# Weight tiles of a two-layer diffusion step: one pump for loads and low parts, and projections' first units loaded inside attention and convolution

## The chip, the core and the metric

One core of one Trainium2 chip runs the whole program. Its engines run in parallel, each through its own stream of instructions in order: TensorE (PE; its weight loads are PEld in the profile), VectorE (DVE), ScalarE (ACT), GpSimd (POOL) and SyncE (SP). POOL and SP also issue DMAs: a DMA that adds to what lies in its destination is issued from POOL. The metric is the device time of one execution in microseconds; lower is better.

## What is computed

Two groups of tokens, 128 of context and 512 of latents, go through two layers; the kernel lays them side by side as 640 columns, features on partitions. A layer is a half-step SwiGLU, a token mixer and a second half-step SwiGLU, each modulated before and normalised after. The mixer of layer 0 is attention (16 query heads, 4 key heads, rotary positions, a window for the latents and a sink), that of layer 1 a Hyena long convolution of order 2.

```python
for i in range(DEPTH):                       # 2 layers
    x = layer_norm(ALPHA*x + 0.5*gate2*swiglu(modulate(x, ...), w1, w2))
    out = attention(modulate(x, ...)) if i % 2 == 0 else hyena(modulate(x, ...))
    x = layer_norm(ALPHA*x + gate5*out)      # out ends in a projection, w_o or w_out
    x = layer_norm(ALPHA*x + 0.5*gate8*swiglu(modulate(x, ...), w1, w2))
# swiglu: (silu(g) * u) @ w2 with g, u = split(h @ w1), inner width 2816
# hyena: h @ w_in (3 parts), short convolution, two long convolutions by FFT, z @ w_out
```

## The kernel before

**Products.** float32 accuracy is had from three products of a faster format (fp32r): a matrix is split into a high part (its rounding) and a low part (the rest), and W x becomes Wh xh + Wh xl + Wl xh. Lines 513 to 524 (`mm_cols`) and 550 to 576 (`ffn1`) issue them in that order, so that the third matmul of every unit is the first that reads the unit's low part. The columns go in two halves of 320.

**Units.** The weights stream through 170 units of 128 partitions and 1 MB (some 768 KB), numbered in the order of use: first feed-forward stage 0 to 35, wqkv 36 to 41 (three for queries, 39 the keys, 40 queries again, 41 the values), wo 42 to 45, feed-forward 46 to 81 and 82 to 117, Hyena input 118 to 129, Hyena output 130 to 133, feed-forward 134 to 169. A feed-forward stage opens with a group of three units (w1) in the order U, U+1, U+2 on half 0 and the same on half 1, and closes with a group of three (one of w1, two of w2b). Between them a w1 unit takes two steps, a w2a unit one. The qkv stage and the Hyena input open with a group of three as well; the two output projections run their first unit alone and the other three as a group.

**Tiles.** The pool `wp` has 8 slots of 1 MB. A unit takes one as it is loaded (`w_dma`, line 108, a DMA from POOL's queue) and a second when its low part is made (`w_split`, line 117): ACT writes minus the high part into the new tile, and a DMA from POOL adds the weights to it from HBM. Both slots come free after the unit's last matmul (`w_done`). Attention puts its key tiles `kh` (two slots) and probabilities `p` (three at a time) into the same pool, the convolution its three tables, its spectra, `ew` and some `yh`, `yl`.

**When.** `run_steps` (line 526) calls `w_get(u)` ahead of every step. Before the change `w_get` issues one more low part whenever fewer than `wmax` units (3) are live and the next one lies at most two ahead, and every low part is followed by loads up to two units further. `wmax` is lowered by hand in attention and convolution, and `wlim` bounds which units may be loaded. The kernel keeps a clock of its own, `now`, which only matmuls of steps advance (0.136 us each); it also places the steps of the layer norms (`at`, `run_due`). In attention both wo units 42 and 43 are loaded before the scores, and 42's low part comes in the group of scores N-3 of N = 20. In the convolution (`hyena`, 8 items of some 8 slots, then a last round with the parts of the projection) unit 130 is loaded at item 7 and its low part made after the fifth slot, followed by the loads of 131 and 132. A program of instructions is written by hand in order, so each engine executes its own in the order of the text.

**Around it.** A residual (`resid`) is a VectorE operation that reads the matmul's result, and from the second column tile on a sum on POOL for the layer norm; the rotary step (`rope`) is ACT, VectorE and POOL work on every q and k tile. `w_first` and `w_split_first` (lines 132 and 140) load a unit on SP's queue as float32 and split it with an ACT copy and a VectorE subtraction; before the change only the first units of all use them.

Of the kernel before, what the change touches and what calls it, by code (L numbers as in the profile page):

```python
# [42 lines left out]
class Kernel:  # L43
# [53 lines left out]
    def w_init(self, units):  # L97
        self.units = units
        self.wd = 0
        self.ws = 0  # L100
        self.wlive = set()
        self.wmax = 3
        self.wlim = len(units)
        self.raw = {}
        self.wt = {}

    def w_dma(self, upto):
        nc = self.nc
        while self.wd < min(upto, self.wlim):
            i = self.wd  # L110
            src, shape = self.units[i]
            r = self.wp.tile(shape, F32R, tag="w", name="wh")
            nc.gpsimd.dma_start(out=r, in_=src)  # L113
            self.raw[i] = r
            self.wd += 1

    def w_split(self):
        i = self.ws
        if i >= self.wlim:
            return  # L120
        self.w_dma(i + 1)
        shape = self.units[i][1]
        hi = self.raw.pop(i)
        lo = self.wp.tile(shape, F32R, tag="w", name="wl")
        self.nc.scalar.activation(out=lo, in_=hi.bitcast(F32), func=AF.Copy, scale=-1.0)  # L125
        self.nc.gpsimd.dma_start(out=lo, in_=self.units[i][0], accum_op=ALU.add)  # L126
        self.wt[i] = (hi, lo)
        self.wlive.add(i)
        self.ws += 1
        self.w_dma(i + 3)  # L130

    def w_first(self):

# [14 lines left out]
    def w_get(self, i):  # L148
        while self.ws <= i:
            self.w_split()  # L150
        if len(self.wlive) < self.wmax and self.ws <= i + 2:
            self.w_split()
        return self.wt[i]

    def w_done(self, i):
# [497 lines left out]
    def attn(self, u0):  # L653
# [18 lines left out]
        u = u0  # L672
# [45 lines left out]
                if half:  # L718
                    nc.scalar.activation(out=kp[:, t, :], in_=ps[:, 192:320], func=AF.Copy)

        self.wlim = u + 5
        self.run_steps(self.group_steps([u, u + 1, u + 2], qstep))
        while self.ws < u + 5:
            self.w_split()
        self.wlim = u + 6
        self.w_dma(u + 6)
        kh = [self.wp.tile([P, 2, 896], F32R, tag="w", name="kh") for _ in range(2)]
        for o in (0, 640):
            for t in range(2):
                k_hi(kc[:, t], slice(o, o + P), t)  # L730
                k_lo(kc[:, t], slice(o, o + P), t)
        self.wmax = 2
        self.run_steps(self.group_steps([u + 3], kstep))
        self.run_steps(self.group_steps([u + 4], qstep))
        self.flush("rope")
        nc.sync.dma_start(out=O["nkT"], in_=kp)
        self.wmax = 1
        wh, wl = self.w_get(u + 5)
        self.wlim = u + 8
        self.w_dma(u + 8)  # L740

        def vstep(tt):
            ps = self.ps(name="v")
# [92 lines left out]
        N = len(groups)  # L836
        parts = self.proj_start(u + 6, o, range(KD), (0,))
        for n in range(N + 2):
            cur = groups[n] if n < N else None
            old = groups[n - 2] if 2 <= n else None  # L840
            nch = len(WIN[old[0]][3]) if old else 0
            for i in range(4):
                if i < nch:
                    tr(*old, i)
                if cur:
                    score(*cur, i)
                if n < 2 and 1 <= 4 * n + i < 6:
                    vstep(4 * n + i - 1)
                if 1 <= n <= N:
                    for j in ((0,), (1, 2), (3,), ())[i]:  # L850
                        norm(*groups[n - 1], j)
                if len(late) > 1 or late and not i < nch:
                    av(*late.pop(0))
                if i < nch:
                    late.append((*old, i))
            if n == N - 3:
                self.wlim = u + 8
                self.w_split()
            if n >= N:
                parts[n - N]()  # L860
        for x in late:
            av(*x)
        self.wmax = 3
        self.wlim = len(self.units)
        self.w_dma(u + 8)
        return self.proj(u + 6, o, gt, 0, 1, ())


# [95 lines left out]
    def spectra(self):  # L964
# [9 lines left out]
        NI = 20  # L974
# [201 lines left out]
                self.clk(2.0)  # L1176
            on(store, r)
        self.wlim = len(self.units)
        self.w_dma(5)
        for seq in range(2):  # L1180
            iv = self.invn[:, seq]
            nc.vector.tensor_scalar(out=iv, in0=iv, scalar1=1e-6, scalar2=None, op0=ALU.add)
# [12 lines left out]
    def hyena(self, u0):  # L1195
# [62 lines left out]
        NI = len(items)  # L1258
# [193 lines left out]
        for u in range(u0, u0 + 12):  # L1452
# [2 lines left out]
            if u < u0 + 3:  # L1455
                continue
            if u == u0 + 8:
                self.wmax = 2
                table_p()
                fold(0, 0)  # L1460
                fold(0, 1)
            for q, s in enumerate(self.group_steps([u], ustep)):
# [3 lines left out]
                if u == u0 + 10:  # L1466
                    if q == 0:
                        table(1)
                    else:
                        self.wmax = 1  # L1470
                        table(2)
                        ld(0)
                        ldp(0)
# [6 lines left out]
        u = u0 + 12  # L1480
        self.h = None
        gt = self.gate(1, 5, 1.0)
        for n in range(NI + 1):
# [19 lines left out]
                ldx(n, 1)  # L1503
            if n == NI - 1:
                self.wlim = len(self.units)
                self.w_dma(u + 1)
            for i, f in enumerate(seq):
                slot(f)
                if n == NI - 1 and i == 4:
                    self.w_split()  # L1510
                if n + 2 < NI and len(seq) - i in (1, 3):
                    fold(n + 2, (3 - len(seq) + i) // 2)
            if n + 1 < NI:
                ldp(n + 1)
        for _ in range(4):
            slot(lambda: None)
        self.wmax = 3
        return self.proj(u, zs, gt, 1, 1, (5, 6, 7))

    def proj_start(self, u, z, early, halves=(0, 1)):  # L1520
# [248 lines left out]
```

## Time and profile before

| | |
|---|---|
| median of three runs | 2763.8 us (2759.21 to 2764.94) |
| the profiled execution | 2762.43 us, span 2760.7 us |
| TensorE busy | 2659.5 us (96%), 17402 matmuls |
| VectorE, ScalarE, GpSimd busy | 1312.3, 889.9, 724.7 us |
| mean granted TensorE clock | 0.986 |
| HBM read | 437.27 MB, 164 GB/s over the span |

The busy share of TensorE is not its share of the peak, since overlapping matmuls count as they lie. What counts for a change of the weight schedule are the places where it stands: the list of waits says for whom, windows say how full the other engines are there, and the timeline of one engine says what stands in front of an instruction in its own queue.

### The profile page before, as it was taken

The numbers are of one execution on the slowest core, as the hardware profiler recorded it, in microseconds if no ns is written. First come the engines' busy times: TensorE is split into PE (matmuls) and PEld (weight loads), VectorE is DVE, ScalarE is ACT, GpSimd is POOL, SyncE is SP. The second block draws the span as 40 slices with busy tenths as digits, with TensorE's granted clock in tenths as the row PEclk, the third lists the DMA queues.
The fourth block names the chain that finished last, engine by engine and source line by source line (L and its number), as shares of the span: only waits on it lengthen the run. The fifth ranks groups of instructions, "written<-read, shape, count | busy, mean of one in ns | idle before, by whom it ended". The sixth has DMA issues, their size and how long they took to land.

```text
span 2760.7 us, 42541 instructions
## 1 busy us (share of the span) xinstructions
PE 2659.5 (96%) x17402; PEld 2525.1 (91%) x17402; DVE 1312.3 (48%) x2893; ACT 889.9 (32%) x1518; POOL 724.7 (26%) x982
## 2 busy tenths in 40 slices
PE   8889999999899999999999999999999899999997
PEld 3679999999745999999999999999999789999997
DVE  6745555627863446555555311117349734211114
ACT  4662222125675332222242222215323333221222
POOL 4421211224213412212142111114119642111113
PEclk9999999999999999999999999999999999999998
DMA  7667988854303569797847756554653365656561
GB/s 244 200 196 206 272 220 246 229 146 115 86 1 88 156 168 266 199 258 218 243 114 203 208 131 166 142 146 124 176 164 125 119 159 132 168 130 176 126 164 54
DMA packets 91946, 461.27 MB, mean 167 GB/s; under 512 B 10991, under 2 KB 16703, under 8 KB 57576
## 3 DMA queue, kind: packets, MB, share of 16 engines
q0 software_dynamic: 71424, 407.60, 56.1%
q1 hardware_dynamic: 19960, 50.92, 5.4%
q8 instruction: 137, 2.24, 0.3%
q14 instruction: 57, 0.47, 0.0%
q10 hardware_dynamic: 368, 0.04, 0.0%
HBM read 437.27 MB, written 16.01 MB: 164 GB/s over the span
## 4 chain that ended last, share of the span: by engine, by line
PE 59%; issue 18%; DVE 6%; POOL 6%; DMA 3%; ACT 2%; SPq 0%; POOLq 0%; DVEq 0%; ACTq 0%
PE f L522 17%; PE g L561 16%; PE u L561 15%; PE u L522 6%; PE o L814 2%; POOL ar L241 1%; POOL wh L113 1%; PE pt L803 1%; DMA wl<-w 1%; POOL wl L126 1%; DVE q L682 1%; DVE yl L1377 1%; PE s L779 1%; PE s L780 0%; DVE p L1348 0%
## 5 line engine op out<-in xcount | busy, mean ns | idle before, releaser
L125 ACT ACTIVATE wl<-wh 128x2048 fp32r<-128x2048 f32 (+1 forms) x168 | 299.5, 1783 | 453.4 <-PE f L522 360.2
L561 PE MATMUL g<-hh,wl 128*128 128x320 f32 (+1 forms) x1408 | 436.1, 310 | 3.3 <-DMA wl<-w 3.3
L522 PE MATMUL f<-al,wh 128*128 128x320 f32 (+2 forms) x1408 | 435.7, 309 | 2.1 <-DVE al L94 1.6
L561 PE MATMUL g<-hh,wh 128*128 128x320 f32 (+1 forms) x1408 | 437.8, 311 | 0.0
L522 PE MATMUL f<-ah,wh 128*128 128x320 f32 (+2 forms) x1408 | 436.6, 310 | 0.0
L522 PE MATMUL f<-ah,wl 128*128 128x320 f32 (+2 forms) x1408 | 435.2, 309 | 1.4 <-DMA wl<-w2b 0.7
L561 PE MATMUL g<-hl,wh 128*128 128x320 f32 (+1 forms) x1408 | 436.0, 310 | 0.0
L561 PE MATMUL u<-hl,wh 128*128 128x320 f32 (+1 forms) x1408 | 435.9, 310 | 0.0
L561 PE MATMUL u<-hh,wl 128*128 128x320 f32 (+1 forms) x1408 | 435.8, 310 | 0.0
L561 PE MATMUL u<-hh,wh 128*128 128x320 f32 (+1 forms) x1408 | 435.8, 310 | 0.0
L571 DVE TENSOR_TENSOR ac<-sg,u 128x320 f32<-128x320 f32 (+1 forms) x176 | 85.7, 487 | 676.0 <-ACT sg L569 675.9
L503 DVE SCALAR_TENSOR_TENSOR x<-f,gate,x 128x128 f32<-128x128 f32 (+3 forms) x432 | 173.5, 435 | 322.1 <-PE f L522 321.6
L569 ACT ACTIVATE sg<-g 128x320 f32<-128x320 f32 (+1 forms) x176 | 76.9, 437 | 761.4 <-PE g L561 755.5
L561 PEld LDWEIGHTS g<-hh,wl 128*128 128x128 f32 x1408 | 265.0, 188 | 3.8 <-DMA wl<-w 3.8
L522 PEld LDWEIGHTS f<-al,wh 128*128 128x128 f32 x1408 | 264.4, 188 | 3.9 <-DVE al L94 3.7
L522 PEld LDWEIGHTS f<-ah,wl 128*128 128x128 f32 x1408 | 264.4, 188 | 1.9 <-DMA wl<-w2b 1.0
L561 PEld LDWEIGHTS g<-hl,wh 128*128 128x128 f32 x1408 | 264.9, 188 | 1.2 <-POOL hl L318 0.5
L561 PEld LDWEIGHTS g<-hh,wh 128*128 128x128 f32 x1408 | 265.1, 188 | 0.5
L522 PEld LDWEIGHTS f<-ah,wh 128*128 128x128 f32 x1408 | 264.4, 188 | 1.0 <-ACT ah L93 0.5
L561 PEld LDWEIGHTS u<-hl,wh 128*128 128x128 f32 x1408 | 265.0, 188 | 0.0
L561 PEld LDWEIGHTS u<-hh,wh 128*128 128x128 f32 x1408 | 265.0, 188 | 0.0
L561 PEld LDWEIGHTS u<-hh,wl 128*128 128x128 f32 x1408 | 265.0, 188 | 0.0
(315 smaller groups left out, 4684.3 us busy)
## 6 DMA issues: line engine op xcount, KB each, us to landing
wh<-w POOLq DMA_DIRECT2D x86, 1024.0 KB, 11.2
wl<-w POOLq DMA_DIRECT2D x86, 1024.0 KB, 9.3
ar<-ada_w POOLq DMA_DIRECT2D x128, 512.0 KB, 6.0
wh<-w2a POOLq DMA_DIRECT2D x48, 768.0 KB, 10.8
wl<-w2a POOLq DMA_DIRECT2D x48, 768.0 KB, 9.2
wh<-hyin POOLq DMA_DIRECT2D x12, 1024.0 KB, 10.7
wl<-hyin POOLq DMA_DIRECT2D x12, 1024.0 KB, 8.1
wr<-ada_first SPq DMA_DIRECT2D x8, 1024.0 KB
```

The source lines that it names most:

```text
L113: nc.gpsimd.dma_start(out=r, in_=src)
L125: self.nc.scalar.activation(out=lo, in_=hi.bitcast(F32), func=AF.Copy, scale=-1.0)
L126: self.nc.gpsimd.dma_start(out=lo, in_=self.units[i][0], accum_op=ALU.add)
L241: self.nc.gpsimd.dma_start(out=self.ada_raw[n], in_=self.I["ada_w"][l, m, j])
L503: nc.vector.scalar_tensor_tensor(out=self.x[:, j, s0:s1], in0=ps[:, s0 - a:s1 - a], scalar=gate[:, tk, j:j + 1], in1=self.x[:, j, s0:s1], ...
L522: nc.tensor.matmul(ps[:, 0:z - a], s[:, kw, c0:c0 + P], m[:, a:z], start=(first and i == 0 and q == 0), stop=(last and i == n - 1 and q == 2))
L561: nc.tensor.matmul(o[:, 0:z - a], s[:, k, c0:c0 + P], m[:, a:z], start=(k == 0 and q == 0), stop=(k == 7 and q == 2))
L569: nc.scalar.activation(out=sg, in_=g[:, 0:z - a], func=AF.Silu)
L571: nc.vector.tensor_tensor(out=ac, in0=sg, in1=uu[:, 0:z - a], op=ALU.mult)
L682: nc.vector.tensor_tensor(out=tiles[r][R[1 - r], c], in0=x[R[r]], in1=tiles[r][R[r], c].bitcast(F32), op=ALU.subtract)
L779: nc.tensor.matmul(ps[:, 0:n], x, kh[t][:, r, c0:c0 + n], start=True, stop=False)
L814: nc.tensor.matmul(ob[R[r], :], v[:, vs[c], g * 64:(g + 1) * 64], pts.pop((b, g, c)), start=(c == 0), stop=(c == len(vs) - 1))
```

## The change

A method `w_pump` takes the place of the fixed rule in `w_get` and of the loads behind each low part. Called once in every `w_get(i)`, it issues at most one low part, of the next unit that is loaded, if that is at most three ahead of i, if slots are left (`wcap`, 8, in attention 6) and if its load was issued at least 7.0 ago on the kernel's clock; then at most one load, of a unit at most four ahead, if after it a slot for the next low part is left. `wmax` is gone. In attention the unit limits open earlier: all units up to 41 at once, 42 and 43 are loaded in the score groups 1 and 3, 42's low part is made in group 5 and 43's in the last one, N-1, with the load of 44. In the convolution unit 130 is loaded by `w_first` on SP's queue and split by `w_split_first` after the fourth slot of item 7, followed by the load of 131; 131's low part is made in the last round after the second part, followed by a load of 132 if it has not been loaded.

```diff
@@ -99,7 +99,8 @@
         self.wd = 0
         self.ws = 0
         self.wlive = set()
-        self.wmax = 3
+        self.wcap = 8
+        self.wcast = {}
         self.wlim = len(units)
         self.raw = {}
         self.wt = {}
@@ -112,6 +113,7 @@
             r = self.wp.tile(shape, F32R, tag="w", name="wh")
             nc.gpsimd.dma_start(out=r, in_=src)
             self.raw[i] = r
+            self.wcast[i] = self.now
             self.wd += 1
 
     def w_split(self):
@@ -127,7 +129,15 @@
         self.wt[i] = (hi, lo)
         self.wlive.add(i)
         self.ws += 1
-        self.w_dma(i + 3)
+
+    def w_pump(self, i):
+
+        used = 2 * len(self.wlive) + len(self.raw)
+        if self.ws in self.raw and self.ws <= i + 3 and used < self.wcap and self.now - self.wcast[self.ws] >= 7.0:
+            self.w_split()
+            used += 1
+        if self.wd <= i + 4 and used + bool(self.raw) < self.wcap:
+            self.w_dma(self.wd + 1)
 
     def w_first(self):
 
@@ -148,8 +158,7 @@
     def w_get(self, i):
         while self.ws <= i:
             self.w_split()
-        if len(self.wlive) < self.wmax and self.ws <= i + 2:
-            self.w_split()
+        self.w_pump(i)
         return self.wt[i]
 
     def w_done(self, i):
@@ -718,26 +727,22 @@
                 if half:
                     nc.scalar.activation(out=kp[:, t, :], in_=ps[:, 192:320], func=AF.Copy)
 
-        self.wlim = u + 5
+        self.wlim = u + 6
         self.run_steps(self.group_steps([u, u + 1, u + 2], qstep))
         while self.ws < u + 5:
             self.w_split()
-        self.wlim = u + 6
         self.w_dma(u + 6)
+        self.wcap = 6
         kh = [self.wp.tile([P, 2, 896], F32R, tag="w", name="kh") for _ in range(2)]
         for o in (0, 640):
             for t in range(2):
                 k_hi(kc[:, t], slice(o, o + P), t)
                 k_lo(kc[:, t], slice(o, o + P), t)
-        self.wmax = 2
         self.run_steps(self.group_steps([u + 3], kstep))
         self.run_steps(self.group_steps([u + 4], qstep))
         self.flush("rope")
         nc.sync.dma_start(out=O["nkT"], in_=kp)
-        self.wmax = 1
         wh, wl = self.w_get(u + 5)
-        self.wlim = u + 8
-        self.w_dma(u + 8)
 
         def vstep(tt):
             ps = self.ps(name="v")
@@ -853,16 +858,20 @@
                     av(*late.pop(0))
                 if i < nch:
                     late.append((*old, i))
-            if n == N - 3:
-                self.wlim = u + 8
+            if n in (1, 3):
+                self.wlim = u + 7 + n // 2
+                self.w_dma(self.wlim)
+            if n == 5:
                 self.w_split()
+            if n == N - 1:
+                self.w_split()
+                self.wlim = len(self.units)
+                self.w_dma(u + 9)
             if n >= N:
                 parts[n - N]()
         for x in late:
             av(*x)
-        self.wmax = 3
-        self.wlim = len(self.units)
-        self.w_dma(u + 8)
+        self.wcap = 8
         return self.proj(u + 6, o, gt, 0, 1, ())
 
 
@@ -1176,7 +1185,7 @@
                 self.clk(2.0)
             on(store, r)
         self.wlim = len(self.units)
-        self.w_dma(5)
+        self.w_dma(4)
         for seq in range(2):
             iv = self.invn[:, seq]
             nc.vector.tensor_scalar(out=iv, in0=iv, scalar1=1e-6, scalar2=None, op0=ALU.add)
@@ -1455,7 +1464,6 @@
             if u < u0 + 3:
                 continue
             if u == u0 + 8:
-                self.wmax = 2
                 table_p()
                 fold(0, 0)
                 fold(0, 1)
@@ -1467,7 +1475,6 @@
                     if q == 0:
                         table(1)
                     else:
-                        self.wmax = 1
                         table(2)
                         ld(0)
                         ldp(0)
@@ -1503,18 +1510,21 @@
                 ldx(n, 1)
             if n == NI - 1:
                 self.wlim = len(self.units)
-                self.w_dma(u + 1)
+                self.w_first()
             for i, f in enumerate(seq):
                 slot(f)
-                if n == NI - 1 and i == 4:
+                if n == NI - 1 and i == 3:
+                    self.w_split_first()
+                    self.w_dma(u + 2)
+                if n == NI and i == 1:
                     self.w_split()
+                    self.w_dma(u + 3)
                 if n + 2 < NI and len(seq) - i in (1, 3):
                     fold(n + 2, (3 - len(seq) + i) // 2)
             if n + 1 < NI:
                 ldp(n + 1)
         for _ in range(4):
             slot(lambda: None)
-        self.wmax = 3
         return self.proj(u, zs, gt, 1, 1, (5, 6, 7))
 
     def proj_start(self, u, z, early, halves=(0, 1)):
```

`w_first` and `w_split_first`, which the convolution now calls:

```python
    def w_first(self):
        i = self.wd
        src, shape = self.units[i]
        self.raw[i] = self.wp.tile(shape, F32, tag="w", name="wr")
        self.nc.sync.dma_start(out=self.raw[i], in_=src)
        self.wd += 1

    def w_split_first(self):
        i = self.ws
        hi, lo = (self.wp.tile(self.units[i][1], F32R, tag="w", name="w" + q) for q in "hl")
        self.split(hi, lo, self.raw.pop(i))
```

## Rows read from the trace of the kernel before

**Rows 1.** What TensorE waited for over the whole span: line and result that waited, what ended it, us in total, times, longest.

```profile
PE f L522 <- DMA wl<-hyout: 12.0, 3, 6.9
...
PE f L522 <- DMA wl<-wo: 5.7, 2, 5.4
...
PE vp L370 <- DVE sq L364: 3.5, 1, 3.5
...
PE g L561 <- DMA wl<-w: 3.3, 2, 2.8
...
PE v L748 <- DMA wl<-wqkv: 3.0, 1, 3.0
PE k L522 <- DMA wl<-wqkv: 2.4, 1, 2.4
```

**Rows 2.** Windows: stretch, its length, busy time of PE, PEld, DVE, ACT and POOL with their instructions, granted TensorE clock, DMA share, GB/s. The first lies in a feed-forward stage, the second in the key projection.

```profile
400.00:450.00 50.00, 50.00 (x343) 50.00 (x342) 30.43 (x57) 10.29 (x10) 10.63 (x17) 1.00 0.95 264
710.00:720.00 10.00, 10.00 (x70) 10.00 (x69) 9.76 (x26) 6.49 (x14) 2.42 (x3) 1.00 0.21 37
```

**Rows 3.** Windows with the same columns: the stretches at half clock behind the waits for wl<-hyout (the first two), wl<-wo, wl<-w and the layer norm's statistics (vp).

```profile
2190.14:2196.96 6.82, 3.57 (x13) 3.57 (x14) 0.83 (x1) 0.74 (x1) 1.36 (x1) 0.50 1.03 341
2220.86:2224.27 3.41, 3.21 (x12) 3.21 (x13) 0.00 (x0) 0.08 (x1) 0.00 (x0) 0.50 1.11 315
893.07:899.90 6.83, 3.87 (x14) 3.87 (x15) 0.00 (x0) 0.00 (x0) 2.00 (x3) 0.50 1.04 275
954.51:964.75 10.24, 9.42 (x37) 9.42 (x38) 3.33 (x8) 3.01 (x8) 2.13 (x5) 0.50 0.19 78
654.14:660.97 6.83, 6.62 (x29) 6.65 (x30) 6.29 (x25) 2.69 (x6) 1.18 (x1) 0.50 0.01 2
```

**Rows 4.** Timeline of PE, start, duration, engine, line, operation, result and operands: the first matmul of the opening group at the feed-forward stage from 1415, the Hyena input, the last feed-forward stage, the qkv stage and the feed-forward stage behind attention.

```profile
1415.45 0.31 PE L561 MATMUL g<-hh,wh 128*128 128x320 f32 x1
...
1886.48 0.31 PE L522 MATMUL u<-hh,wh 128*128 128x320 f32 x1
...
2268.70 0.31 PE L561 MATMUL g<-hh,wh 128*128 128x320 f32 x1
...
638.02 0.31 PE L522 MATMUL q<-hh,wh 128*128 128x320 f32 x1
...
936.84 0.31 PE L561 MATMUL g<-hh,wh 128*128 128x320 f32 x1
```

**Rows 5.** Timeline of POOL: the issue of the low part's DMA that stands in the program at the first step of four of these groups, and in one of them the sum right before it.

```profile
1420.38 0.88 POOL L510 TENSOR_TENSOR sum<-sum,x 128x320 f32<-128x320 f32 x1
1421.20 0.88 POOL L126 DMA_DIRECT2D wl<-w  x1
...
1892.22 0.88 POOL L126 DMA_DIRECT2D wl<-hyin  x1
...
2273.48 0.89 POOL L126 DMA_DIRECT2D wl<-w  x1
...
643.75 0.87 POOL L126 DMA_DIRECT2D wl<-wqkv  x1
```

**Rows 6.** DMA issues, each line from a window around one issue: tiles, queue, count, KB, us from issue to landing. They are the issue at 1421.20, that at 1892.22, that at 942.90 (three other loads were issued in the 1.6 us before it), and the plain load at 2173.16.

```profile
wl<-w POOLq DMA_DIRECT2D x1, 1024.0 KB, 8.2
...
wl<-hyin POOLq DMA_DIRECT2D x1, 1024.0 KB, 8.0
...
wl<-w POOLq DMA_DIRECT2D x1, 1024.0 KB, 12.4
...
wh<-hyout POOLq DMA_DIRECT2D x1, 1024.0 KB, 5.1
```

**Rows 7.** From the groups of instructions of ACT by shape, the low part's copy of a 1 MB unit (count, busy us, mean ns, idle before); and from the timeline of ACT the end of the first unit's activation in the groups from 1415 and from 937.

```profile
L125 ACT ACTIVATE wl<-wh 128x2048 fp32r<-128x2048 f32 x120 | 228.7, 1906 | 357.4 <-PE f L522 304.2 <-DMA wh<-w 30.7 <-DMA wh<-wo 12.9
...
1429.66 0.47 ACT L93 ACTIVATE ah<-ac 128x320 fp32r<-128x320 f32 x1 [2.24 <-DVE ac L571]
...
950.16 0.47 ACT L93 ACTIVATE ah<-ac 128x320 fp32r<-128x320 f32 x1 [0.84 <-DVE ac L571]
```

**Rows 8.** Timelines ahead of the scores: DVE's first score, and ACT's copies of the cached keys.

```profile
736.68 0.61 DVE L782 CUSTOM_DVE_ANT_0 p<-s,mask,sinkn 128x384 f32<-128x384 f32 x1
...
696.29 4.89 ACT L687 ACTIVATE kh<-kc 64x128 fp32r<-64x128 f32 x15
```

**Rows 9.** Timelines in the attention output: DVE's residual of unit 42 on half 1, and POOL's sum of it.

```profile
882.77 0.68 DVE L503 SCALAR_TENSOR_TENSOR x<-f,gate,x 128x192 f32<-128x192 f32 x2 [2.85 <-PE f L522]
...
889.20 1.19 POOL L508 TENSOR_TENSOR sum<-x 128x320 f32<-128x320 f32 x1
```

**Rows 10.** The end of the convolution: PE's wait for unit 130's low part; ACT's evacuation and DVE's operations around the place where the split is put; the last one of DVE's convolution work; the fifth z tile; and the subtraction of `w_split_first` (here of units 0 and 1: min, median and max ns).

```profile
2193.39 0.64 PE L522 MATMUL f<-zh,wl 128*128 128x320 f32 x1 [6.88 <-DMA wl<-hyout]
...
2180.07 0.37 ACT L1422 ACTIVATE yy<-ivp,invn 128x128 f32<-128x128 f32 x1 [0.37 <-PE ivp L1414]
...
2179.82 0.47 DVE L1426 SCALAR_TENSOR_TENSOR yy<-iv,invn,yy 128x256 f32<-128x256 f32 x1
...
2185.20 0.86 DVE L1443 TENSOR_TENSOR zl<-yy,zh 128x640 fp32r<-128x640 f32 x1
...
2189.43 0.69 DVE L1377 TENSOR_TENSOR yl<-y,yh 128x512 fp32r<-128x512 f32 x1
...
L94 DVE TENSOR_TENSOR wl<-wr,wh x2: 2292/2292/2292, 148.9 to 155.4; 128x2048 fp32r<-128x2048 f32 x2
```

## The prediction

> **What bounds the kernel now.** I read the list of TensorE's waits first, then windows of the engines, then single moments of each engine around the waits. In a feed-forward stage TensorE has no hole: 50.00 of 50 us busy, 343 matmuls, 0.146 us each [rows 2]. So every unit there costs its matmuls and a better weight schedule can win nothing, but can lose. What TensorE waits for is in the list [rows 1]: low parts of weight tiles at the Hyena output projection (12.0 us), the attention output projection (5.7), the first feed-forward units behind it (3.3), the value (3.0) and key (2.4) projections. That is 26.4 us, 1% of the span, and the change is about it. Behind a wait stands a second price: for some us the granted clock is 0.50, 1.2 instead of 2.4 GHz [rows 3]. TensorE's busy time in such a stretch, halved, is what it cost: 1.8 us behind the 6.9 us wait, 1.6, 1.9, 4.7 and 3.3 behind the others. For a new wait I take 1.8.
>
> **How far ahead a low part must start.** A step (one unit, one half, 48 matmuls) is 7.0 us for TensorE. A low part is an ACT copy (1.9 us, [rows 7]) and an accumulating 1 MB DMA from POOL, 8.0 to 8.2 us from issue to landing where nothing stands before it [rows 6]: over 10 us, more than one step, less than two. The third matmul of a unit reads it.
>
> **The opening groups of three units (U, U+1, U+2).** Before, U+1's low part is issued at the last step of the group before, U+2's at the first step of its own: two steps ahead. After, I count slots and the kernel's clock by hand. In the closing group of a feed-forward stage the next unit U gets its low part at the third step, all 8 slots are then full, U+1 is loaded only at the fifth step and U+2 at the sixth. At the sixth, U+1's load is one step old: 8 x 6 x 0.136 = 6.528 on the kernel's clock, under the 7.0 that `w_pump` asks. So U+1's low part goes out at U's first step and U+2's at U+1's first step: one step ahead each. This happens at four openings (qkv, the first and the last feed-forward stage of layer 1, Hyena input); behind attention it hits only the third unit. Where in time those program places lie can be read now, since before issues another unit's low part at the same place.
> - First feed-forward of layer 1: the group starts at 1415.45 [rows 4]; POOL issues at 1421.20, behind the sums of the closing residual [rows 5], landing 8.2 later, 1429.4. U+1's third matmul is due at 1415.45 + 7.0 + 0.6 (statistics matmuls, two matmuls) = 1423.1: a wait of 6.3. U+2's copy stands on ACT behind the activation that ends at 1430.1 [rows 7]: 1430.1 + 1.9 + 0.3 + 8.2 = 1440.5. TensorE goes on there at 1440.5 instead of 1430.6: **+9.9**. Ends: +6.3 (no second wait, no slow clock) and +11.5.
> - Hyena input: start 1886.48, issue 1892.22, landing 1900.2, due 1894.1: wait 6.1, clock 1.8, no second wait: **+7.8** (5 to 9, the low end because half 1 of this group may have slack).
> - Last feed-forward: start 2268.70, issue 2273.48, landing 2281.5, due 2276.3: wait 5.2; U+2's at 2293.6 by the same distance from the start as above: **+9.8** (5 to 11.5).
> - qkv: start 638.02, issue 643.75, landing 651.8, due 645.9: wait 5.9 and 1.8 of clock, in the place of 3.5 [rows 1] and 3.3 [rows 3] for the layer norm, whose statistics are then ready: +0.9.
> - First feed-forward behind attention: before, the third unit waits 2.8 us of the 3.3, its DMA needing 12.4 because of three loads ahead [rows 6], and 4.7 of clock. After, its load is 6.528 old at the first step, so the copy comes one step later, behind the activation that ends at 950.6 [rows 7]: 950.6 + 1.9 + 0.3 + 8.0 = 960.8, due 951.8: wait 9.0 + 1.8 against 7.5: **+3.3** (0 to +6.2, the slow stretch gone or unchanged).
>
> **Key and value projections.** Their low parts get three and four steps instead of two; both waits go, 2.4 + 3.0 [rows 1], and an estimated 1.7 of clock, as behind the smaller waits of [rows 3]. But VectorE is busy 9.76 of 10 us here [rows 2] with the rotary work and reaches the first score only at 736.68 [rows 8]; the TensorE work won would wait for it. Worth 0 then; 7.1 if that cover were not there. Unit 40's copy (1.9 us) moves to just before ACT's key copies at 696.29 [rows 8], for which VectorE waits in line: +1.9. With qkv: **+2.8** (-4.5 to +4.5).
>
> **Attention output.** Unit 42 and 43 are ready early. They cost nothing: two slots that the scores do not need, and a copy on ACT two groups ahead of its reader; without that cover 1.9 us. Unit 44's load is again 6.528 old at the projection's start, so its low part stands on POOL behind the second residual's sum: residual done 883.45, sum 1.19 [rows 9], issue 884.7, landing 892.7 to 894; due at 889.9. The wait of 5.4 becomes 2.8 to 4.1: **-2.1** (-3 to +1; unit 45, one step ahead too, may wait 2).
>
> **Hyena output.** Removed from the path: unit 130's accumulating DMA and TensorE's wait of 6.9 for it [rows 1]. Added: a load on SP's queue, behind the last spectrum loads, 5.1 us on an idle queue [rows 6] and so in time; an ACT copy of 1.9 and a VectorE subtraction of 2.29 [rows 10]. On ACT the copy follows the evacuation that ends at 2180.44; VectorE, in order and without a gap here, stops from 2179.82 until 2184.65 (2180.44 + 1.9 + 2.29), so its chain is 4.8 later: the fifth z tile, before at 2186.1, comes at 2190.9, the last convolution part, before at 2190.1, at 2194.9. TensorE is at 130's third matmul at 2193.39 - 6.88 = 2186.5, runs on to the tenth behind it, 2188.0, and waits there 2.9 for that z tile; by the time it has done both parts and the first terms of the next inverse product (2190.9 + 0.4 + 2.2 + 1.3) the convolution part is there. Units 131 and 132 come with low parts issued at the last round and the projection's start, some 10 us ahead of use each: the other waits go too. Gone: 12.0 of waits [rows 1], 1.8 and 1.6 of clock [rows 3], 15.4; new: 2.9, and 1.7 for a slow stretch behind it: **-11** (-16 if VectorE's delay is hidden, -5 if 131, queued behind loads of 132 and 133, is late too). Were POOL also held for the 2.29, its last product would end as much later: -8.7. The Trainium skill, "SBUF — State Buffer", section "SBUF: two separate sides", says that a VectorE operation with two SBUF inputs and a GpSimd operation that reads SBUF exclude each other for a whole instruction. By it the term would be that -8.7; no row here separates such a lock from waits in order, and the sum goes without it.
>
> **Steady state.** Low parts still start 2 to 4 steps ahead, with one raw tile less in stock. Nothing waits there now, 14 us ahead is enough by the sums above: 0, and up to +3 over all stages if unit 50, 86 or 122 (two steps) meet a full queue.
>
> **Sum.** 2.8 - 2.1 + 3.3 + 9.9 + 7.8 + 9.8 - 11.0 = +20.5, made against the profiled execution, 2762.43 (span 2760.7 and 1.7 around it): 2782.9. The median of the runs is 1.4 above it: **2784**.
>
> **Rivals.**
> - Faster: the opening waits do not arise because POOL issues the low parts when TensorE begins the group, not 5.7 us later behind the sums. They would land at about 1423.7, due 1423.1. Then only the gains stay: -11 - 2.1 - 7.5 + 1.9 = -18.7, **2745**. It decides at an issue some 6 us earlier. Against it: in the row shown POOL's issue comes right behind a sum [rows 5], the others as long after their group's start, and program order does not change there.
> - A DMA that lands quickly: with 5.1 us as the plain load on an idle queue [rows 6], first waits shrink by 3 and second ones vanish: openings +5, +4.9, +4, the others about 0, sum about -2: **2762**. Against: accumulating DMAs took 8.0 even alone. The Trainium skill, "DMA: Bandwidth & Descriptors", section "Anatomy of one DMA", has 2.0 us and bytes / 436e3 for one: an estimate of 4.4 us for 1 MB; the rows disagree with it.
> - The Hyena end wins nothing, since the subtraction holds VectorE's chain and unit 131 queues behind 132 and 133: **2795**.
> - VectorE's cover of the key and value waits is thin and they pay: -7.1, **2777**.
>
> **How the numbers follow.** Forecast 0.52, thin cover 0.15, no gain at Hyena 0.13, quick landing 0.08, openings in time 0.12. Slower by over 0.2% (what measurement tells from no change, 5.5 us) takes the forecast, thin cover and no gain, less 0.04 for tails: 0.76. Same: 0.10. Faster: 0.14. The range leaves out the fast rival and thin tails: 2760 to 2800, the upper end being all openings at their dear ends.
>
> **What would show it.** Right: a wait of 5 to 6.5 us for a low part in the second unit of each of the four openings, one of 9 in the third unit behind attention; no wait at 130 for its low part but one of some 3 for a z tile; no wait at key and value, yet the first score no earlier. Wrong: openings without waits, or low parts landing in 5 us; or a step in the feed-forward middle that waits.

## The result: slower by 40 us, twice what was forecast

| | before | after |
|---|---|---|
| median | 2764.4 us (4 runs, 2759.2 to 2766.8) | 2804.9 us (4 runs, 2802.4 to 2806.8) |
| ratio after to before | | 1.0148, interval 1.0131 to 1.0166 |
| span of the profiled execution | 2760.7 us | 2802.7 us |
| TensorE busy | 2659.5 us | 2672.1 us |
| mean granted TensorE clock | 0.986 | 0.981 |

The sign was forecast, the size was not: 2784, with 2800 as the upper end.

TensorE's waits in the kernel after, the same view as [rows 1] (result that waited, what ended it, us in total, times, longest):

```profile
PE g L570 <- DMA wl<-w: 26.0, 6, 8.1
...
PE f L531 <- ACT ah L93: 8.2, 2, 4.4
PE q L531 <- DMA wl<-wqkv: 6.1, 2, 5.3
...
PE u L531 <- DMA wl<-hyin: 4.9, 2, 3.8
PE o L819 <- ACT pts L810: 3.9, 3, 2.5
...
PE v L753 <- DVE sm L787: 3.7, 1, 3.7
PE f L531 <- DMA wl<-wo: 3.6, 2, 2.2
```

The reader is to set this beside [rows 1]. The 12.0 for wl<-hyout and the waits of key and value for low parts have left the list. The 3.3 for wl<-w have become 26.0, hyin is new, and so is a row that no step of the prediction had: 8.2 us for `ah`, an activation and not a weight.

**Where in time.** Both kernels issue the same 17402 matmuls in the same order, so the start of one matmul can be set against its start in the other kernel. These are the five group starts of [rows 4] in the kernel after (PE's timeline); U, U+1 and U+2 are, as in the prediction, the units of an opening group:

```profile
646.91 0.31 PE L531 MATMUL q<-hh,wh 128*128 128x320 f32 x1
...
950.25 0.31 PE L570 MATMUL g<-hh,wh 128*128 128x320 f32 x1
...
1435.73 0.31 PE L570 MATMUL g<-hh,wh 128*128 128x320 f32 x1
...
1919.96 0.31 PE L531 MATMUL u<-hh,wh 128*128 128x320 f32 x1
...
2296.36 0.31 PE L570 MATMUL g<-hh,wh 128*128 128x320 f32 x1
```

They are late by 8.9, 13.4, 20.3, 33.5 and 27.7 us against [rows 4], and the span by 42.0. The differences of these are the time lost in each stretch; the same was worked out for some of the experiments below, each from its own five starts and span against those of before:

| stretch | forecast | after | stock2 | age65 | load_first | close_late | best1 |
|---|---|---|---|---|---|---|---|
| up to the qkv stage | 0 | +8.9 | -1.2 | +49.2 | +0.9 | +7.4 | +0.6 |
| qkv, scores, attention output | +0.7 | +4.5 | +4.8 | +5.4 | +11.3 | +3.8 | -4.3 |
| feed-forward behind attention | +3.3 | +6.9 | -1.5 | +42.5 | +6.8 | +11.1 | -1.3 |
| first feed-forward of layer 1 | +9.9 | +13.2 | 0.0 | +12.5 | +10.7 | +19.2 | 0.0 |
| Hyena input to Hyena output | -3.2 | -5.8 | -13.9 | -5.3 | -4.2 | -5.7 | -12.1 |
| last feed-forward stage to the end | +9.8 | +14.4 | +1.4 | +8.3 | +11.5 | +18.5 | +1.4 |
| sum | +20.5 | +42.1 | -10.4 | +112.6 | +37.0 | +54.3 | -15.7 |

**The closing groups.** The first stretch lost 8.9 us where nothing was forecast. Its own end shows it. ACT's timeline there (start, duration, line, operation; in brackets the idle time before it and what ended it):

```profile
604.34 1.91 ACT L127 ACTIVATE wl<-wh 128x2048 fp32r<-128x2048 f32 x1 [8.76 <-DMA wh<-w2b]
606.16 0.42 ACT L578 ACTIVATE sg<-g 128x320 f32<-128x320 f32 x1
607.13 0.47 ACT L93 ACTIVATE ah<-ac 128x320 fp32r<-128x320 f32 x1 [0.55 <-DVE ac L580]
```

POOL's timeline at the same place, and PE's:

```profile
593.11 0.87 POOL L128 DMA_DIRECT2D wl<-w2b  x1 [11.20 <-ACT wl L127]
593.83 0.70 POOL L114 DMA_DIRECT2D wh<-w2b  x1
606.55 0.87 POOL L128 DMA_DIRECT2D wl<-w2b  x1 [12.02 <-ACT wl L127]
607.10 0.87 POOL L114 DMA_DIRECT2D wh<-wqkv  x1
```

```profile
607.65 0.63 PE L531 MATMUL f<-ah,wh 128*128 128x320 f32 x1 [4.44 <-ACT ah L93]
```

The load issued at 593.83 lands at 604.3 (10.5 us). ACT has stood 8.76 us for it at the copy of 604.34, with the activation `sg`, `ah` of the closing group behind it. The low part's DMA waits on POOL for that copy until 606.55, and the next load stands behind the low part, 607.10. So one load, one copy and one issue follow each other, 13.3 us for one unit, and no load is under way while a copy is made. Before, the next load was under way while the copy was made, and a copy in a feed-forward stage hardly waited for its load: 30.7 us over the whole run in [rows 7]. The same groups of ACT in the kernel after (busy, mean ns, idle before and what ended it):

```profile
L127 ACT ACTIVATE wl<-wh 128x2048 fp32r<-128x2048 f32 x119 | 227.1, 1910 | 619.0 <-DMA wh<-w 514.7 <-DMA wh<-w2b 39.2 <-PE f L531 31.9
...
L127 ACT ACTIVATE wl<-wh 128x1536 fp32r<-128x1536 f32 x48 | 71.2, 1483 | 195.5 <-DMA wh<-w2a 159.0 <-PE f L531 26.4 <-issue 10.1
```

The loads named there add up to 713 us of ACT standing. The Trainium skill, "PSUM — Partial Sum Buffer", section "Engine vs sequencer instructions", says that "ScalarE/VectorE/GpSimdE queues are strict FIFO"; the two timelines agree, with 8.76 us on one queue and 12.02 on the other.

**The openings.** PE's timeline at the first and the last feed-forward stage of layer 1:

```profile
1448.62 0.64 PE L570 MATMUL g<-hh,wl 128*128 128x320 f32 x1 [4.85 <-DMA wl<-w]
...
1460.79 0.42 PE L570 MATMUL g<-hh,wl 128*128 128x320 f32 x1 [3.54 <-DMA wl<-w]
...
2307.55 0.41 PE L570 MATMUL g<-hh,wl 128*128 128x320 f32 x1 [3.17 <-DMA wl<-w]
...
2320.98 0.63 PE L570 MATMUL g<-hh,wl 128*128 128x320 f32 x1 [4.59 <-DMA wl<-w]
```

Windows over the stretches at half clock behind waits in the kernel after, with the columns of [rows 2] (the first is the closing above, the others lie behind the waits just shown):

```profile
605.09:611.92 6.83, 4.27 (x15) 4.03 (x16) 1.53 (x3) 1.96 (x3) 1.42 (x2) 0.50 0.60 106
...
1448.18:1451.59 3.41, 2.97 (x11) 2.97 (x12) 1.95 (x5) 1.71 (x2) 0.00 (x0) 0.50 0.39 151
1461.84:1468.67 6.83, 6.83 (x31) 6.81 (x30) 2.44 (x14) 0.00 (x0) 0.00 (x0) 0.50 0.76 148
2308.34:2311.75 3.41, 3.41 (x15) 3.41 (x14) 2.43 (x5) 1.23 (x2) 0.21 (x1) 0.50 0.22 84
2318.58:2328.83 10.25, 7.85 (x33) 7.84 (x34) 2.43 (x14) 0.43 (x1) 0.88 (x1) 0.50 0.71 135
```

Half of TensorE's busy time is what the clock cost, at most: 1.5 + 3.4 = 4.9 us at the first of the two openings, 1.7 + 3.9 = 5.6 at the second. With the waits that is 8.4 + 4.9 = 13.3 and 7.8 + 5.6 = 13.4; by the starts of the same matmuls the two openings lost 12.9 and 13.0. The low part's issue at the first of them, on POOL, comes right behind a sum as in [rows 5], 4.0 us behind the group's start:

```profile
1438.91 0.88 POOL L519 TENSOR_TENSOR sum<-sum,x 128x320 f32<-128x320 f32 x1
1439.73 0.90 POOL L128 DMA_DIRECT2D wl<-w  x1
```

**The end of the convolution**, PE and DVE (compare [rows 10]):

```profile
2228.06 0.41 PE L531 MATMUL f<-zh,wh 128*128 128x320 f32 x1 [1.24 <-ACT zh L1449]
...
2229.80 0.63 PE L531 MATMUL f<-zl,wh 128*128 128x320 f32 x1 [1.33 <-DVE zl L1452]
```

```profile
2221.09 2.61 DVE L94 TENSOR_TENSOR wl<-wr,wh 128x2048 fp32r<-128x2048 f32 x1 [0.84 <-ACT wh L93]
```

VectorE is held by the wait for the copy and by the subtraction, but for less than forecast. Its next operation, at 2179.82 in [rows 10], comes at

```profile
2223.63 0.47 DVE L1435 SCALAR_TENSOR_TENSOR yy<-iv,invn,yy 128x256 f32<-128x256 f32 x1
```

which is 43.81 us later, of which 40.35 were brought along: 3.5 for the 4.8 of the prediction. TensorE waits for the z tiles (1.24 and 1.33), and no low part is late. By the starts of the same matmuls this stretch won 12.7. Of these, 1.5 are in no term of the prediction: the kernel before ran at a granted clock of 0.50 from 2176.48 to 2179.90, and the kernel after does not at that place.

```profile
2176.48:2179.90 3.42, 3.42 (x19) 3.42 (x18) 3.42 (x7) 1.10 (x2) 3.24 (x5) 0.50 0.63 232
```

### The profile page after: what moved, and what is told of

Read it like the earlier page. It is cut to its first block, busy times and chain, and to the rows that moved or that the text cites. A ratio compares the mean times of both kernels' runs of the same rounds, so it can differ in the third digit from the quotient of the medians.

```text
span 2802.7 us, 42563 instructions
## 1 busy us (share of the span) xinstructions
PE 2672.1 (95%) x17402; PEld 2534.9 (90%) x17402; DVE 1315.6 (47%) x2894; ACT 889.4 (32%) x1518; POOL 723.1 (26%) x980
## 4 chain that ended last, share of the span: by engine, by line
PE 68%; issue 12%; DVE 6%; POOL 4%; DMA 3%; ACT 2%; POOLq 0%; DVEq 0%; ACTq 0%
PE f L531 21%; PE g L570 18%; PE u L570 18%; PE u L531 6%; PE o L819 2%; PE pt L808 1%; DMA wl<-w 1%; POOL wh L114 1%; POOL ar L250 1%; DMA wh<-w2b 1%; DVE yl L1386 1%; PE s L784 1%; POOL wl L128 1%; DVE q L691 0%; DVE p L1357 0%
## 5 line engine op out<-in xcount | busy, mean ns | idle before, releaser
L128 POOL DMA_DIRECT2D wl<-w x86 | 75.5, 878 | 654.9 <-ACT wl L127 597.1
```

## The experiments

Two theories went into them. **The chain:** the pump leaves room for one load only, so that each load is issued behind the low part before it and each copy waits for its load; the stock of the steady state (units loaded whose low part is not yet made) runs down and the end of a stage pays. **The age:** the threshold of 7.0 against a step of 6.528 puts off the low parts at the openings, as the prediction had it.

**stock2.** One condition of the kernel after:

```diff
-        if self.wd <= i + 4 and used + bool(self.raw) < self.wcap:
+        if self.wd <= i + 4 and used < self.wcap:
```

> The kernel after, with one condition cut: a load no longer has to leave a slot for the next low part, so that two loads can be in stock or under way (as before the change) and not one. Theory of the chain: in the kernel after nearly every low part's copy waits on ACT for a load that was issued right behind the low part before it, one unit per 12.4 to 13.1 us, and what stands behind that copy on ACT waits with it. With two loads under way the copies find their weights: the waits for ah in the closing groups (4.4 and 3.8 us, with their clock 7.2 and 4.2) go. By the count of steps U+1 and U+2 are then also loaded two steps earlier, so that the opening waits go too (13.1, 6.9 and 13.4, and some 2 behind attention): 2804.9 - 11.4 - 35.4 = 2758, within 5. Rival, the age alone (the 7.0 asked against a step of 6.528 puts off every low part): the threshold is unchanged here, so the openings stay and the time is 2793 to 2805. Rival, the transfers themselves have become slower because more of them are under way at once: the closings stay, 2770 or more.

2753.5 us, ratio to before 0.9963 (0.9949 to 0.9977), 51 us less than the kernel after. The ACT groups again, and the wait for weights of the feed-forward stages:

```profile
L127 ACT ACTIVATE wl<-wh 128x2048 fp32r<-128x2048 f32 x119 | 226.8, 1906 | 345.2 <-PE f L531 313.3 <-DMA wh<-w 29.7 <-DMA wh<-wo 2.2
...
L127 ACT ACTIVATE wl<-wh 128x1536 fp32r<-128x1536 f32 x48 | 70.8, 1476 | 96.0 <-PE f L531 56.0 <-issue 40.0
```

```profile
PE g L570 <- DMA wl<-w: 3.0, 1, 3.0
```

ACT stands 32 us for loads in place of 713, the losses at closings and openings are gone (table; the 3.0 that is left stands at the place of the 3.3 of [rows 1]), and the age is unchanged. So the room for one load carries both losses; the age alone makes no opening late. The rival of slower transfers is refuted with it.

**age65.** The kernel after with `>= 7.0` made `>= 6.5`.

> The kernel after with the age that a load must have before its low part lowered from 7.0 to 6.5, just under a step of 6.528. Theory of the age for the openings: the low parts of U+1 and U+2 go out one step earlier at all four openings and of the third unit behind attention, and the waits there with their clock go: 13.1, 6.9, 13.4, some 2 behind attention and 2 at qkv, 2804.9 - 37 = 2768. The theory of the chain says that the closings are not helped by it: a load still follows the low part before it, the waits for ah of 4.4 and 3.8 us stay or grow, 2768 to 2775. Rival: the opening waits come from the single load in stock alone; the copy then only stands earlier on ACT and waits there for its load, and the time stays near 2800.

2875.9 us: both theories missed it by 100, and the rival, near 2800, by 76. Its mechanism, a copy that only stands earlier on ACT and waits there, is what the waits and ACT groups show:

```profile
PE f L531 <- ACT ah L93: 69.1, 13, 9.8
...
PE g L570 <- DMA wl<-w: 9.8, 4, 3.9
```

```profile
L127 ACT ACTIVATE wl<-wh 128x2048 fp32r<-128x2048 f32 x119 | 227.5, 1912 | 904.3 <-DMA wh<-w 706.8 <-DMA wh<-hyin 73.9 <-DMA wh<-w2b 56.8
...
L127 ACT ACTIVATE wl<-wh 128x1536 fp32r<-128x1536 f32 x48 | 71.3, 1486 | 336.9 <-DMA wh<-w2a 326.3 <-PE f L531 10.6
```

The opening waits did shrink (26.0 to 9.8, and none for wqkv is left), as the age theory said. But with one load at a time an earlier copy only stands on ACT the longer: of ACT's idle time in these groups 1164 us now end with a load, and thirteen times TensorE waits for an activation behind such a copy, in the middle of stages too. In this chain the 7.0 had been protection: of two ills it was the lesser one.

**load_first and load_first65.** In the kernel after, the load of one call is issued ahead of its low part, all conditions kept; the second kernel has 6.5 for 7.0 as well.

```diff
-        if self.ws in self.raw and ... >= 7.0:
-            self.w_split()
-            used += 1
-        if self.wd <= i + 4 and used + bool(self.raw) < self.wcap:
-            self.w_dma(self.wd + 1)
+        low = self.ws in self.raw and ... >= 7.0
+        if self.wd <= i + 4 and used + low + bool(len(self.raw) - low) < self.wcap:
+            self.w_dma(self.wd + 1)
+        if low:
+            self.w_split()
```

> The kernel after with the two steps of w_pump changed over: the load of one call is issued ahead of its low part, not behind it. Slots, age and the step of every issue are those of after. Theory of the chain: a load then no longer stands on POOL behind a low part whose copy waits for the load before, two loads are under way, and the closings (7.2 and 4.2 us) go; the openings, which hang on the step at which the program issues U+1's and U+2's low parts, keep their waits (13.1, 6.9, 13.4): 2804.9 - 11.4 = 2793, 2788 to 2797. Rival, the slots alone hold the loads back (one load in stock): the order on POOL does nothing, 2800 to 2808. Second rival, the openings too come from late loads: about 2762.

> load_first with the age lowered from 7.0 to 6.5. With the low part first this made the kernel 71 us slower, since its copies stood on ACT waiting for loads. Theory: the age does harm only by that chain; with the load first it sets the openings, which get their low parts one step earlier: 2793 - 33 = 2760, 2755 to 2775. Rival, an age of one step is too short for a transfer of 8 to 10 us in any order, since a step takes 7: copies wait on ACT again, 2830 to 2880.

2798.2 us (2795.1 to 2802.4), 6.7 less than after and between the ranges of the theory and its rival, and 2773.9 (2766.5 to 2778.0), inside the theory's. load_first, waits:

```profile
PE g L570 <- DMA wl<-w: 23.8, 4, 8.3
...
PE q L531 <- DMA wl<-wqkv: 9.3, 2, 8.3
...
PE f L531 <- DMA wl<-w2b: 2.5, 1, 2.5
```

The order on POOL alone takes away all waits for `ah`, and the first closing's loss with them (8.9 to 0.9 in the table). The second closing was not won: it waits for a w2b low part instead, the qkv opening got dearer, 9.3 for 6.1, and the attention output's wait for `wo` grew from 3.6 to 5.5. The trace tells the two closings apart by the landing of the last unit's low part: at the first it was issued at 596.29 with no load just ahead of it and landed in 7.9 us; at the second it was issued at 1390.10, half a us behind a load of the next stage, and took 11.9, up to the end of TensorE's wait at 1402.0. So the chain theory is right on the first closing and was half right on the sum; the load ahead has a price of its own. With the age at 6.5 the order decides over 102 us (2875.9 against 2773.9): most of that age's harm comes with the order of two issues in one call. Not all: in load_first65 TensorE waits for `ah` again, 9.8 us in four, and the kernel is still slower than before, by a ratio of 1.0038 (1.0024 to 1.0052).

**close_late.** In the closing groups of the kernel after, the pump is called behind the first step, so that the copy stands on ACT behind `sg` and `ah`:

```diff
+                    if n:
+                        step(self.w_get(q))
+                    else:
+                        step(self.wt[q])
+                        self.w_pump(q)
```

> The kernel after with one thing moved: in the closing group of each feed-forward stage the pump is called behind the first step and not ahead of it, so that on ACT the low part's copy, which waits for its load, stands behind that step's activation (sg, ah) and not ahead of it. Loads, their order on POOL and the one load in stock are those of after. Theory of the held queue: the second matmul step waits for ah only because the copy holds ACT; the waits for ah (4.4 and 3.8 us) go with their slow clock, 7.2 and 4.2: 2804.9 - 11.4 = 2793.5, 2790 to 2797; the openings stay. Rival: the closing steps wait for their weights, which come late in this kernel, and the wait for ah only hides a wait for a low part of about the same length: 2800 to 2808.

2814.7 us, 10 more than after. The theory of the held queue is refuted; the rival has the mechanism, but its range, 2800 to 2808, was too low as well:

```profile
PE f L531 <- DMA wl<-w2b: 18.0, 6, 6.0
...
PE f L531 <- ACT ah L93: 0.5, 1, 0.5
```

The waits for `ah` are gone but for 0.5, and 18.0 us of waits for the same units' low parts stand in their place, and at more places. ACT's copies of the last unit's low part, in the first closing and in that of the first stage of layer 1:

```profile
601.98 1.92 ACT L127 ACTIVATE wl<-wh 128x2048 fp32r<-128x2048 f32 x1 [1.89 <-DMA wh<-w2b]
...
1884.06 1.90 ACT L127 ACTIVATE wl<-wh 128x2048 fp32r<-128x2048 f32 x1
```

In the first closing ACT is free and the copy still waits 1.89 for its load: there the held queue was the form of the loss, and its cause is that the load comes late. In layer 1 the copy has its load and stands behind `ah`; it comes 4.3 us later than in the kernel after (1877.80, with 2.0 brought along). So what this kernel loses at the closings of layer 1, which were spared in the kernel after, is the price of its own edit.

**hyena_only.** The kernel before with the Hyena part alone.

> The kernel before with the Hyena part of the change alone: unit 130 loaded on SP's queue at item 7 and split by ACT and VectorE after the fourth slot, 131 and 132 brought forward. By the prediction's term (-11) and by how TensorE's matmuls in the kernel after stand against those of before over this stretch (-12.7): 2764.4 - 12 = 2752. Rival: part of what was won there was time that an earlier delay had put into slack, or comes only with the new pump: 2758 to 2764.

2754.3 us, ratio 0.9962 (0.9947 to 0.9977): 10 us won without the pump.

**score_only.** The kernel before with the part inside the score groups alone.

> The kernel before with only what the change does inside the score groups: units 42 and 43 loaded in groups 1 and 3, low parts of 42 in group 5 and of 43 in the last one with the load of 44. Theory: each copy of 1.9 us stands on ACT ahead of the score groups' copies pts, for which TensorE waits, and is paid: +1.8 and +1.1; the output projection wins some 4: 2764.4 - 1 = 2763. Rival: the 8.7 us that the kernel after has lost between the start of qkv and that of the output projection come from these groups alone: 2769 or more.

2763.7 us, ratio 0.9997 (0.9988 to 1.0006), as expected. Its waits:

```profile
PE o L812 <- ACT pts L803: 3.9, 3, 2.5
...
PE f L522 <- DMA wl<-wo: 2.1, 1, 2.1
```

The copy of group 5 is paid by TensorE (the 2.5, a wait for `pts`), and the attention output's 5.7 of [rows 1] fall to 2.1: one pays for the other.

**kv_early.** The kernel before, with the value projection's unit loaded in the first qkv group and its low part made one group earlier (`wlim` at u + 6 from the start, no `wmax = 2`).

> The kernel before with the value projection's unit loaded inside the first qkv group and its low part made ahead of the second query group (limit 3 live units kept instead of 2), nothing else. TensorE's wait of 3.0 us for it, and some 1.7 behind it, go. Theory of the cover: VectorE, full with the rotary work up to the first score, decides; its first score comes no earlier (a copy in front of its operands may cost up to 1.9): 2764.4, 2763 to 2767. Rival, thin cover: TensorE keeps what it wins, 2764.4 - 4.7 = 2759.7.

2767.5 us, ratio 1.0010 (1.0001 to 1.0020).

```profile
PE v L746 <- DVE sm L780: 5.0, 1, 5.0
```

The wait for the low part (3.0) is gone and the wait for VectorE's `sm` has grown from 1.2 to 5.0. VectorE's first score starts at 738.92, at 736.68 before [rows 8]; of these 2.2 us, 1.2 lie ahead of the qkv stage. That is cover, as forecast. The time is 0.5 above the range that was expected: the attention output's wait for `wo` has grown from 5.7 to 7.4, which nothing here foresaw.

**stock2_65 and best1.** stock2 with the age 6.5; best1 besides with unit 42's low part in score group N-3 and not 5.

> The kernel with room for two loads (2753.5), and the age 6.5 instead of 7.0. By the count of steps only the low parts of units 44 and 45 in the attention output come earlier by it, where 4.2 us of waits are left: 2749 to 2753. Rival, the age does harm by itself: 2770 or more.

> stock2_65 with the low part of unit 42 made in the score group N-3, where the kernel before made it, and not in group 5. Theory: in group 5 the copy stands ahead of pts and costs 1.8; at N-3 ACT has slack: 1.8 less than stock2_65, 2747 to 2751. Rival: a copy of 1.9 us costs the same in every group: as stock2_65.

2747.7 (ratio 0.9940, 0.9925 to 0.9954) and 2746.4 us (0.9936, 0.9921 to 0.9951). With room for two loads the lower age is a gain: the waits for `wo`, 4.2 us in stock2, are no longer in the list. best1's own step:

```profile
PE o L819 <- ACT pts L810: 2.1, 3, 0.8
```

The wait for `pts` falls from 3.9 to 2.1, the 1.8 expected; in the medians the two can't be told apart. best1 is 18 us faster than before and 58 faster than after.

## Why the prediction was wrong, step by step

- **Steady state: the step that failed.** "Low parts still start 2 to 4 steps ahead, with one raw tile less in stock. Nothing waits there now ...: 0, and up to +3." The steps were counted in the program's text. In it a low part is 2 steps behind its load, but the load stands on POOL behind the low part before, whose copy waits for the load before that: one unit per 12.6 to 13.4 us at the end of the first stage, where the closing group wants three units in three steps of 7. Measured: 7.2 us at the first closing (0.70 for a w2b low part, 4.44 for `ah`, 2.1 of clock) and 4.3 at that of the feed-forward stage behind attention. The missing tile, named in that sentence and priced at nothing, is what stock2 gives back. Of the 21.5 us by which the sum fell short, these closings are 11.5, the two-wait openings 6.2 and the scores 5.4; the rest is small and nearly cancels.
- **Openings: the mechanism as forecast, the sum mis-sized.** Each wait came where it was placed. U+1's low part was issued 4.0 us behind the group's start where 5.7 was taken from [rows 4, 5], and the waits were shorter: 8.4 in two for 9.9, 7.8 for 9.8, 4.9 for 6.1 at Hyena input, 8.05 for 9.0 behind attention. But the clock was left out of the two-wait openings, "For a new wait I take 1.8" being applied to the single ones alone: by the starts of the same matmuls +9.9 became +12.9 and +9.8 became +13.0. Hyena input lost 6.9 for 7.8 (its 6.1 and 1.8 add up to 7.9), the opening behind attention 2.4 for 3.3. That the age against the step makes them was only half the cause: the units are loaded that late because of the same condition.
- **qkv: right.** VectorE reached its first score at 748.84, 12.2 later than before [rows 8], of which 8.9 were brought along: +3.3 against +2.8. In VectorE's chain stands a wait of 1.70 for the copy in front of the cached keys, forecast at 1.9. That a removed wait is worth nothing under this cover, kv_early shows by itself for the value's; for the key's it is not shown apart.
- **Scores: cover that was not there.** "They cost nothing: ... a copy on ACT two groups ahead of its reader; without that cover 1.9 us." Unit 42's copy cost 1.8 and unit 43's 1.1, and the first score groups another 2.5 by the starts of the same matmuls, at the half clock (0.50 from 748.45 to 755.28) behind TensorE's wait of 3.7 for `sm`: +5.4 for 0. The attention output won 3.8 for 2.1.
- **Hyena output: right, the number in part by luck.** -12.7 for -11. The wait behind VectorE's delay was 2.6 in two against 2.9, but the delay itself was 3.5 and not 4.8. The 1.5 of the slow stretch that was gone belong to no term, and best1 and stock2_65, with the same Hyena part, have such a stretch; without it the gain is 11.2. By the lock that the Trainium skill states ("SBUF — State Buffer", section "SBUF: two separate sides") the term would have been -8.7; the measured gain lies on the side of the sum without it. It does not decide on the lock: POOL had one instruction left as the subtraction began, until 2221.56, and then no operation until 2225.69.
- **The rest.** TensorE's first feed-forward matmul was 1.3 us late already, in a part that the change does not touch and that moved by 0.0 to +3.8 in the other runs. Another 1.4 was lost at the end; hyena_only, stock2 and best1 show the same 1.4, kv_early and score_only none, so it comes with the Hyena part. Its form is a stretch at a granted clock of 0.50 (2775.97 to 2779.38 in the kernel after) with no wait of TensorE above 0.54 in the 75 us before; the kernel before has none there. What brings it I did not find.

None of the rivals came about. The thin cover and the accumulating DMA that lands in 5 us were refuted (kv_early; 7.8 to 8.8 us at the openings too).

What stays open: why the closings of the two stages of layer 1 were spared in the kernel after. The trace shows how, not why: in the first stage of layer 1 the last unit's low part was issued 0.9 us ahead of the group's first w2b matmul, at the two closings that lost 7.2 and 4.3 it was issued 5.8 and 4.2 behind it.

## What to carry to other kernels

A prefetch has two leads, that of the work made from a load and that of the load itself; where both are issued from one queue in order, the load's lead is what counts, and one tile less in stock can turn an overlapped pair into a chain. Count leads in the order of each engine's queue and not in steps of the text, and look at what each waiting instruction holds behind it. Price a wait of TensorE with the half clock behind it, every wait and not only the first: here it added 40 to 70% to the waits of the closings and of the openings with two waits.

## What was not expected of the hardware

Each transfer was faster in the slower kernel: over the stretch 440 to 600 us the median load of 1 MB landed in 9.9 us and the median low part in 8.0, against 12.2 and 10.4 in the same stretch before, and 12.4 and 10.7 in stock2, which has room for two loads as well. That it comes of less being in flight is likely, and not shown by itself. The DMA issues of that stretch after the change (count, KB, median us to landing):

```profile
wh<-w POOLq DMA_DIRECT2D x7, 1024.0 KB, 9.9
wl<-w POOLq DMA_DIRECT2D x7, 1024.0 KB, 8.0
```

A profile page that shows shorter transfers can belong to the slower kernel.
